# Attention probabilities: the far high parts copied behind the exponentials, and no work held back behind the last unit

## The chip, the cores and the metric

The kernel runs on one core of one Trainium2 chip. Its metric is the device time of one execution in microseconds. Before the change three timed executions gave 1129.56, 1130.15 and 1130.64 us; their median, 1130.15 us, is the time before. The core's engines are TensorE (PE for products and transposes, PEld for its weight loads), VectorE (DVE), ScalarE (ACT), GpSimd (POOL) and SyncE (SP, which issues most DMAs).

## The reference, cut to what matters

One encoder layer over 1024 tokens of width 1024, batch 1, in float32. It begins with an RMSNorm and one projection into a pooling part (512 columns) and queries, keys and values of 8 heads of 64. The change lies in the chunked attention:

```python
def one_chunk(args):
    c, qb = args                                   # 64 queries; keys: own chunk and 8 before
    s = jnp.einsum('bqhd,bkhd->bhqk', qb, kb).astype(jnp.float32) * scale + bias
    s = jnp.where(valid[None, None, None, :], s, -jnp.inf)
    pr = jax.nn.softmax(s, axis=-1).astype(vb.dtype)
    return jnp.einsum('bhqk,bkhd->bqhd', pr, vb)
```

Behind it come the output projection with its residual, a gated MLP (width 2816, with a causal convolution), a gated per-layer embedding and a last RMSNorm; none of these is touched.

## The kernel before, in words

**Precision.** Every product of two float32 operands is made of three products of reduced ones: an operand is split into a high part (a rounding copy on ACT) and a low part (the operand less its high part, on DVE), and high x high, high x low and low x high are summed in PSUM (`mm3`, lines 136 to 138; `split`, lines 141 and 142). Here "copy" means the making of a high part and "remainder" the making of a low part.

**Units.** Attention runs per pair of heads (4 pairs) and per unit of query tiles of 128 tokens. A pair has 6 units: tiles 0 to 2 together, then tiles 3, 4, 5, 6 and 7 alone, so there are 24 units. A tile sees up to 5 key tiles; the units have 6, 4, 5, 5, 5 and 5 key tiles.

**Visits.** `unit(u)` is called for u = 0 to 24. I call it visit u, and number it within its round of six: visit 0 works on the scores of tiles 0 to 2, visit 1 on tile 3, up to visit 5 on tile 7. On PE a visit issues, in this order:

1. the transposes of the probabilities of unit u-1 (line 441, `probs_t`);
2. the scores of unit u (line 418);
3. steps of a long projection that fills the time (queries and keys of the next pairs, then the pooling columns: `project`, generator `fill`; a step is one `mm3`);
4. in the visits after the last tile of a group (tiles 0 to 2, 3 to 5, 6 and 7), the products of probabilities and values of that group (line 493, `values`). These are visits 1, 4 and 0, and visit 24; the code calls them valued. Visit 0 is also called merged here, since its own unit has three tiles.

**PSUM.** There are 8 banks. Transposed probabilities of the first four key tiles of a unit go to banks 2 and 3, those behind the fourth (the far ones) to banks 6 and 7: two key tiles for the unit of tiles 0 to 2, none for tile 3, one for each of tiles 4 to 7. Scores lie in banks 4 to 7: a tile with four or five key tiles uses all four of them. Projections use banks 0 and 1, the values bank 5 and one of banks 0 and 1.

**ACT and DVE.** Their work of a visit is not issued where it is written. `push(t, fn)` puts it on a list with a time t, and `flush` issues the list in order of t; both engines then work in exactly this order, each through its own queue. Entries that are marked slow (weight splits of the projection and splits of queries and keys) stay on the list when `flush(True)` is called and go out with the next plain `flush()`. The entries are:

- the copy of the transposed probabilities (line 459, ACT) at 0.0 for near, 0.05 for far ones;
- per head and tile the minimum of the negated scores plus bias (lines 383 and 387, DVE) from 1.0 on, the exponential with its sum (line 395, ACT) from 1.9 to 3.3, the reciprocal (line 398, DVE) from about 2.95, and the scaled row (line 391 on ACT for the second head of the pair, from 3.9; line 393 on DVE for the first, from 3.0);
- the remainder of the probabilities (line 461, DVE) at 2.5 (near) and 2.52 (far) in valued visits, at 3.55 and 3.57 in the others;
- the evacuation of a finished projection bank (lines 300 and 584, DVE), at the time it is finished, though not before 3.6 in visits that are not valued;
- slow entries at 5.2 or later (lines 329, 332, 330, 333; weight splits: copy line 529 on ACT, remainder line 527 on DVE or POOL).

The next visit's transposes write the banks that the remainders read, so they follow the remainders of this visit. Within a group the value products take the key tiles in the order wide, narrow, wide and so on, first all high parts, then all low parts; in the group of tiles 3 to 5 the far key tile of tile 5 comes second, in the group of tiles 0 to 2 a far key tile comes second too, in the group of tiles 6 and 7 the far key tile of tile 7 comes fourth.

**The end.** Visit 24 has no unit of its own: it transposes and copies the probabilities of unit 23, issues nine projection steps, then the values of unit 23. Behind them the projection goes on with the second half of the last column block's weights (`weights(ct, 1)`), whose split is a slow entry. The order in which ACT and DVE work is that of the code; the work that follows the attention (output weights, splits of its result) lies partly between. Output weights (line 640, SP) are loaded into the buffers from which the projection weights are split.

Of the kernel before, what the change touches and what calls it, by code (L numbers as in the profile page):

```python
# [8 lines left out]
AF = mybir.ActivationFunctionType  # L9
# [66 lines left out]
NU = len(UNITS)  # L76
PER = NU // (N_HEADS // 2)


def key_tiles(u):  # L80

    return sum(min(t + 1, BANDT) for t in UNITS[u][1]) if 0 <= u < NU else 0


def group_at(t):

    return next(g for g in GROUPS if g[0] <= t < g[1])


def is_last(u):  # L90

    t = UNITS[u][1][-1]
    return t + 1 == group_at(t)[1]


def block_at(k, t):

    t0, t1 = group_at(t)
    return t1 * t + k if t0 == 0 else 5 * (t - t0) + k - t + 4 - max(0, 4 - t0)


def trunk(tc, xT, xn, pT, vecs, w_qk0, w_in, w_v, bias, counts, pool_w, w_out, w_up, w_down,
          w_gate, w_ple, out):
    nc = tc.nc
    act, dve, pe, pool, sp = nc.scalar, nc.vector, nc.tensor, nc.gpsimd, nc.sync

    with tc.tile_pool(name="sb", bufs=1) as sb, \
# [23 lines left out]
        def rv(ap):  # L131
            return ap.bitcast(F32)
# [172 lines left out]
        def push(t, *fns, slow=False):  # L305

            for n, fn in enumerate(fns):
                pending.append((t + 0.8 * n, len(pending), fn, slow))

        def flush(part=False):  # L310
            todo = sorted((p for p in pending if not (part and p[3])), key=lambda p: p[:2])
            pending[:] = [p for p in pending if part and p[3]]
            owed.clear()
            for p in todo:
                p[2]()
# [21 lines left out]
        def run_later(n):  # L337
            for fn in later[:n]:
                fn()
            del later[:n]  # L340
# [26 lines left out]
        def load_bias(h):  # L367
            b = biasb[h % 3]
            sp.dma_start(b, bias[h])

            def turned():
                dve.memset(b[0:64, 576:640], -BIG)
                dve.memset(b[64:128, 0:64], -BIG)
            return turned
# [53 lines left out]
        def probs_t(u):  # L428

            c, ts = UNITS[u]  # L430
            total = key_tiles(u)

            def place(x, m):
                n = 2 * m + x
                return (2, HD * n) if n < 8 else (6, 512 + HD * (n - 2 * total))

            for x in range(2):
                for m in range(total):
                    bank, col = place(x, m)
                    for y in range(2):  # L440
                        pe.transpose(PS[:, bank + y, col:col + HD], Sb[x][halves[y], m * P:(m + 1) * P],  # L441
                                     ident[halves[y], halves[y]], tile_position=(HD * y, 0))
            todo, m = [], 0
            for t in ts:
                nk = min(t + 1, BANDT)
                b0 = block_at(t + 1 - nk, t)
                for a, b in ((0, min(nk, 4 - m)), (max(4 - m, 0), nk)):
                    if b > a:
                        bank, col = place(0, m + a)
                        todo.append((b0 + a, b0 + b, bank, PS[:, bank:bank + 2, col:col + 2 * HD * (b - a)]))  # L450
                m += nk
            return todo

        def probs_out(todo, valued):
            for a, b, bank, ps in todo:
                src = ps.rearrange("p a (n q) -> p n a q", q=HD)
                hi, lo = [pt[:, a:b].rearrange("p k x (a q) -> p (k x) a q", a=2) for pt in PT]
                far = bank > 3
                push(0.05 if far else 0.0, lambda hi=hi, src=src: act.activation(hi, src, AF.Copy))  # L459
                push((2.5 if valued else 3.55) + 0.02 * far,  # L460
                     lambda lo=lo, src=src, hi=hi: dve.tensor_tensor(lo, src, rv(hi), ALU.subtract))  # L461

        credit, turns, valued = 0.0, [], [False]

        def values(u):
            nonlocal credit
            c_, ts = UNITS[u]
            if not is_last(u):
                return
            t0, t1 = group_at(ts[-1])  # L470
            n, by = t1 - t0, 4 if t0 else t1
            while u < NU - 1 and at[0] < 2.3:
                next(fill)
                credit -= 0.5
                now[0] += STEP
            flush(True)
            reach = {k: (max(t0, k), min(t1, k + BANDT)) for k in range(max(0, t0 - 4), t1)}
            wide = [k for k, (a, b) in reach.items() if b - a == n]
            narrow = sorted((k for k in reach if k not in wide), key=lambda k: reach[k][1] - reach[k][0])
            keys = [k for pair in zip(wide, narrow) for k in pair]  # L480
            keys += [k for k in wide + narrow if k not in keys]
            free = (bankn[0] + 1) % 2
            if n == 2:
                bank = free if u < NU - 1 else 5
                Os = [PS[:, bank, 256 * j:256 * j + 256] for j in range(2)]
            else:
                Os = [PS[:, bank, 0:n * P] for bank in (5, free)]
            todo = [(part, k) for part in range(2) for k in keys]
            for j in range(2):
                for n_, (part, k) in enumerate(todo):  # L490
                    a, b = reach[k]
                    b0 = block_at(k, a)
                    pe.matmul(Os[j][:, (a - t0) * P:(b - t0) * P].rearrange("p (t q) -> p t q", q=P), V[:, k, 2 * c_ + j],  # L493
                              PT[part][:, b0:b0 + by * (b - a - 1) + 1:by, j], start=n_ == 0, stop=n_ == len(todo) - 1)
            for j in range(2):
                a = halves[j]
                act.activation(otmp[a, 0:n * P], Os[j][halves[1 - j]], AF.Copy)  # L497
                if n == 2 and j == 0:
                    continue
                for i in range(2) if n == 2 else (j,):  # L500
                    a = halves[i]
                    dve.tensor_tensor(o32[a, c_, t0 * P:t1 * P], Os[i][a], otmp[a, 0:n * P], ALU.add)
                if j == 0:
                    flush()
# [167 lines left out]
        def lay_due(u):  # L672

            for c, x, h in list(qk_ready):
                if u >= (c - 1) * PER + (0 if x else PER - 1 if h else 1):
                    qk_ready.remove((c, x, h))
                    push(max(4.8, now[0] + 0.4), *lay(c, x, h), slow=True)
# [4 lines left out]
        def unit(u):  # L682

            nonlocal credit
            now[0] = 0.0
            unit_at[0] = u
            if u < NU:
                c, ts = UNITS[u]
                for h in range(2 if ts[-1] > 3 else 1):
                    while not all((c, x, h) in laid for x in range(2)):  # L690
                        next(fill)
                        lay_due(u - 1)
                        flush()
            valued[0] = u > 0 and is_last(u - 1)
            if u:
                probs_out(probs_t(u - 1), valued[0])
            if u < NU:
                softmax(scores(u), valued[0])
                if u % PER == PER - 1:
                    for h in (2 * c + 3, 2 * c + 4):  # L700
                        if h < N_HEADS:
                            push(3.0, lambda h=h: turns.append(load_bias(h)))
                lay_due(u)
                credit += ROOM[u % PER]
                now[0] = 1.25
                least = LEAST[u % PER] if u else 0
                while credit >= 1 or least > 0:
                    if valued[0] and credit < 2 and least < 1 and 4.7 < at[0] < 5.4:
                        break
                    now[0] += STEP  # L710
                    credit -= 1
                    least -= 1
                    if next(fill, True) is False:
                        break
                    lay_due(u)
            else:
                for _ in range(DRAIN):
                    now[0] += STEP
                    next(fill)
            if valued[0]:  # L720
                flush(True)
                values(u - 1)
            flush()
            if turns and (u % PER == PER - 1 or u % PER == 1):
                turns.pop(0)()
            run_later(LATER)
# [766 lines left out]
```

## Time and profile before

| what | value |
|---|---|
| timed executions | 1129.56, 1130.15, 1130.64 us; median 1130.15 us |
| the profiled execution's own time | 1126.68 us |
| its span, first to last instruction | 1124.9 us |
| granted TensorE clock | 0.998 |
| busy: PE, PEld, DVE, ACT, POOL | 1109.0, 919.9, 842.8, 579.9, 163.5 us |
| attention, from the first scores to the last values | about 71 to 262 us of the span |

All rows of the trace are of the profiled execution. A row of a timeline has the start in us from the span's beginning, the duration in us, engine, line, operation and operands; in square brackets stands how long the engine had been idle before it and what ended that. A row of waits has the engine, its line, what it waited for, the total in us, the number of times, and the longest. A row of groups has the number of instructions, the total in us and the mean of one in ns.

### The profile page before, as it was taken

The page shows a single profiled execution, that of the slowest core. Times are in us where ns is not written, and L with a number is a line of the kernel's source. Part 1 is how long each engine was busy: PE and PEld are TensorE (multiplying, and loading weights), DVE is VectorE, ACT ScalarE, POOL GpSimd, SP SyncE. Part 2 cuts the span into 40 slices and gives each one's busy share as a digit, 9 for nine tenths or more (in the row PEclk, how much of TensorE's full clock was granted, in tenths as well). Part 3 has the DMA queues.
Part 4 walks back from the last instruction along what each step waited for, and adds up shares of the span by engine and source line. Part 5 has one row for each costly group of instructions (what it writes and reads, how often), then busy time and mean ns, then how long its engine had stood idle before and what let it go on. Part 6 is the DMA issues. An engine that isn't in the chain of part 4 may idle for free.

```text
span 1124.9 us, 15599 instructions
## 1 busy us (share of the span) xinstructions
PE 1109.0 (99%) x5658; PEld 919.9 (82%) x5658; DVE 842.8 (75%) x1449; ACT 579.9 (52%) x1021; POOL 163.5 (15%) x196
## 2 busy tenths in 40 slices
PE   9999999999999999999999999999999999999997
PEld 7888877877888888888888888888888888888887
DVE  6437777777668879887787778778877789986845
ACT  7537766664564544444443444344444544674634
POOL 0000101086002200210112011201120112000000
PEclk9999999999999999999999999999999999999999
DMA  9401111103510352674668465756576556420003
GB/s 346 160 1 38 44 43 39 41 20 129 176 52 10 92 163 92 159 169 131 159 150 177 133 160 140 170 149 159 136 166 157 132 156 133 142 94 20 1 31 119
DMA packets 66172, 129.02 MB, mean 115 GB/s; under 512 B 7600, under 2 KB 9008, under 8 KB 66096
## 3 DMA queue, kind: packets, MB, share of 16 engines
q1 hardware_dynamic: 51840, 102.33, 27.5%
q0 software_dynamic: 13824, 25.17, 13.9%
q8 instruction: 44, 0.72, 0.3%
q10 hardware_dynamic: 432, 0.53, 0.1%
q14 instruction: 32, 0.26, 0.1%
HBM read 113.32 MB, written 14.68 MB: 114 GB/s over the span
## 4 chain that ended last, share of the span: by engine, by line
PE 84%; DVE 7%; ACT 5%; issue 3%; POOL 1%; POOLq 0%; DVEq 0%; ACTq 0%
PE PS L136 26%; PE PS L137 26%; PE PS L138 26%; PE PS L493 3%; ACT F L395 2%; DVE B L461 2%; ACT B L459 1%; DVE F L383 1%; DVE R L142 1%; PE PS L441 1%; PE PS L418 1%; ACT R L141 0%; POOL TB L951 0%; POOL F L941 0%; ACT F L497 0%
## 5 line engine op out<-in xcount | busy, mean ns | idle before, releaser
L136 PE MATMUL PS<-R 128*128 128x512 f32 (+1 forms) x1084 | 420.1, 388 | 0.1
L138 PE MATMUL PS<-R 128*128 128x512 f32 (+1 forms) x1084 | 416.9, 385 | 0.0
L137 PE MATMUL PS<-R 128*128 128x512 f32 (+1 forms) x1084 | 416.9, 385 | 0.0
L136 PEld LDWEIGHTS PS<-R 128*128 128x128 f32 x1084 | 203.6, 188 | 44.0 <-issue 2.9
L138 PEld LDWEIGHTS PS<-R 128*128 128x128 f32 x1084 | 203.6, 188 | 40.8
L137 PEld LDWEIGHTS PS<-R 128*128 128x128 f32 x1084 | 203.7, 188 | 39.5
L141 ACT ACTIVATE R<-F 128x512 fp32r<-128x512 f32 (+2 forms) x220 | 136.6, 637 | 174.6 <-PE PS L137 78.4
L142 DVE TENSOR_TENSOR R<-F,R 128x512 fp32r<-128x512 f32 (+2 forms) x220 | 152.4, 709 | 46.9 <-ACT R L141 45.9
L876 DVE TENSOR_TENSOR F<-F 128x512 f32<-128x512 f32 x88 | 60.7, 690 | 51.1 <-DMA F<-in_w_up 50.3
L1186 DVE TENSOR_TENSOR F<-F,PS 128x512 f32<-128x512 f32 x140 | 92.8, 683 | 6.6 <-PE PS L138 6.4
L141 ACT ACTIVATE BQ<-RW 128x512 fp32r<-128x512 f32 x90 | 52.6, 622 | 76.7 <-PE PS L137 72.5
L1129 POOL DMA_DIRECT2D RW<-Yd x56 | 49.5, 885 | 260.9 <-DMA RW<-Yd 196.9
L1129 POOL DMA_DIRECT2D RW<-in_w_down x40 | 35.9, 945 | 231.6 <-DMA RW<-in_w_down 195.2
L142 DVE TENSOR_TENSOR BQ<-RW,BQ 128x512 fp32r<-128x512 f32 x90 | 59.2, 688 | 2.5 <-PE PS L137 1.7
L137 PE MATMUL PS<-BQ 128*128 128x512 f32 x140 | 54.6, 390 | 0.1
L138 PE MATMUL PS<-BQ 128*128 128x512 f32 x140 | 54.5, 389 | 0.0
L136 PE MATMUL PS<-R,BQ 128*128 128x512 f32 x140 | 54.5, 389 | 0.0
L136 PE MATMUL PS<-BQ 128*128 128x512 f32 x140 | 54.5, 389 | 0.0
L137 PE MATMUL PS<-R,BQ 128*128 128x512 f32 x140 | 54.5, 389 | 0.0
L138 PE MATMUL PS<-R,BQ 128*128 128x512 f32 x140 | 54.5, 389 | 0.0
L1012 ACT ACTIVATE F<-F,vec 128x1024 f32<-128x1024 f32 (+1 forms) x25 | 28.6, 1143 | 48.5 <-DVE F L987 43.6
L395 ACT ACTIVATE F<-F,small 128x640 f32<-128x640 f32 (+4 forms) x64 | 43.9, 689 | 18.2 <-DVE small L383 17.0
(179 smaller groups left out, 1581.3 us busy)
## 6 DMA issues: line engine op xcount, KB each, us to landing
F<-in_w_up SPq DMA_DIRECT2D x91, 256.0 KB, 4.2
RW<-Yd SPq DMA_DIRECT2D x60, 256.0 KB, 3.7
RW<-Yd POOLq DMA_DIRECT2D x56, 256.0 KB, 4.8
RW<-in_w_down SPq DMA_DIRECT2D x50, 256.0 KB, 3.0
RW<-in_w_down POOLq DMA_DIRECT2D x40, 256.0 KB, 6.2
Yd<-F SPq DMA_DIRECT2D x40, 256.0 KB, 3.5
F<-in_w_in SPq DMA_DIRECT2D x10, 512.0 KB, 3.5
F<-in_xn SPq DMA_DIRECT2D x8, 512.0 KB, 7.2
```

Of the source, the lines that this page charges most:

```text
L136: pe.matmul(ps, ahi, bhi, start=first, stop=False, skip_group_check=more)
L137: pe.matmul(ps, ahi, blo, start=False, stop=False, skip_group_check=more)
L138: pe.matmul(ps, alo, bhi, start=False, stop=last, skip_group_check=more)
L141: both = (act.activation(hi, src, AF.Copy), dve.tensor_tensor(lo, src, rv(hi), ALU.subtract))
L142: dve.tensor_tensor(lo, src, rv(hi), ALU.subtract))
L395: push(1.9 + 0.85 * z, lambda S=S, s_=s_: act.activation(S, S, AF.Exp, bias=s_[:, 0:1], scale=-1.0, accum_out=s_[:, 1:2]))
L461: lambda lo=lo, src=src, hi=hi: dve.tensor_tensor(lo, src, rv(hi), ALU.subtract))
L493: pe.matmul(Os[j][:, (a - t0) * P:(b - t0) * P].rearrange("p (t q) -> p t q", q=P), V[:, k, 2 * c_ + j], PT[part][:, b0:b0 + by * (b - a - ...
L876: return dve.tensor_tensor(rawu[to], rawu[a], rawu[b], op)
L1012: act.activation(y, Gb[:, 2 + a:2 + b], AF.Identity, bias=vec[:, C_CB + fi:C_CB + fi + 1], scale=cw(2))
L1129: pool.dma_start(t, src, accum_op=ALU.add)
L1186: dve.tensor_tensor(t, t, PS[:, 4 + d], ALU.subtract if n in (1, 5) else ALU.add)
```

## The change

In `probs_out` the copies and remainders of far probabilities get other times; near ones keep theirs. In a valued visit the far copy moves from 0.05 to 2.92, which is behind both exponentials of a single tile (1.9 and 2.75), and in a merged visit to 2.76, which is behind the fourth of six exponentials (2.75). The far remainder goes from 2.52 to 0.01 behind its copy. In the other visits the far copy moves to 3.5, behind the exponentials and ahead of the scaled row on ACT, and its remainder stays at 3.57. In `values` and in `unit`, the `flush(True)` ahead of the value products becomes a plain flush for the last unit, so that its slow entries are issued ahead of them.

```diff
-        def probs_out(todo, valued):
+        def probs_out(todo, valued, merged):
             for a, b, bank, ps in todo:
                 src = ps.rearrange("p a (n q) -> p n a q", q=HD)
                 hi, lo = [pt[:, a:b].rearrange("p k x (a q) -> p (k x) a q", a=2) for pt in PT]
                 far = bank > 3
-                push(0.05 if far else 0.0, lambda hi=hi, src=src: act.activation(hi, src, AF.Copy))
-                push((2.5 if valued else 3.55) + 0.02 * far,
+                soon = 2.76 if merged else 2.92
+                push(0.0 if not far else soon if valued else 3.5, lambda hi=hi, src=src: act.activation(hi, src, AF.Copy))
+                push((soon + 0.01 if valued else 3.57) if far else 2.5 if valued else 3.55,
                      lambda lo=lo, src=src, hi=hi: dve.tensor_tensor(lo, src, rv(hi), ALU.subtract))
...
-            flush(True)
+            flush(u < NU - 1)
...
-                probs_out(probs_t(u - 1), valued[0])
+                probs_out(probs_t(u - 1), valued[0], u % PER == 0)
...
             if valued[0]:
-                flush(True)
+                flush(u < NU)
                 values(u - 1)
```

The first of the two flushes is in `values(u)`, where u is the unit whose values are made (23 for the last), the second in `unit(u)`, where the last visit is 24.

## The prediction

> **What bounds the kernel now.** I began with the page and the busy time by stage.
>
> ```profile
> span 1124.9 us, 15599 instructions
> ...
> PE 84%; DVE 7%; ACT 5%; issue 3%; POOL 1%; POOLq 0%; DVEq 0%; ACTq 0%
> ```
>
> ```profile
> 71.00:262.00 191.00, 185.01 (x1480) 153.10 (x1478) 136.44 (x349) 127.39 (x268) 47.30 (x63) 1.00 0.13 41
> 262.00:285.00 23.00, 21.38 (x93) 17.41 (x94) 18.69 (x33) 13.42 (x23) 8.56 (x12) 1.00 0.32 103
> ```
>
> In each row stand the stretch, its length, then busy time of PE, PEld, DVE, ACT and POOL, clock, DMA share and GB/s. PE sets the end: 84% of the chain of waits is PE. In the stretch of the attention it is idle for 191.00 - 185.01 = 6.0 us, in the 23 us behind it for 1.6 us. These 7.6 us are all that moving ACT and DVE work can win there, and what PE wins there it should keep, since it is the bound of what follows. The longest waits of the weight loads, and one of DVE, between 55 and 285 us say where the idle time is:
>
> ```profile
> PEld PS L441 <- DVE B L461: 9.2, 12, 1.3
> ```
>
> ```profile
> DVE F L383 <- ACT B L459: 19.6, 16, 3.0
> ```
>
> PE waits for the remainders (L461) when it starts the transposes of a visit (and once behind the last values, shown below). The second row shows who is late before that: the minimum waits for the probability copy 16 times. Sixteen is the number of visits with a far copy and scores that fill banks 4 to 7 (visits 1, 3, 4, 5 in four rounds).
>
> **The far copy and the minimum.** Visit 2 has no far copy; the next visit has one:
>
> ```profile
> 85.92 1.12 PE L418 MATMUL PS<-R 64*128 64x320 f32 x12
> 86.16 1.03 ACT L459 ACTIVATE B<-PS 128x1024 fp32r<-128x1024 f32 x1 [0.16 <-PE PS L441]
> 87.08 0.82 DVE L383 CUSTOM_DVE_ANT_0 F<-PS,F 128x640 f32<-128x640 f32 x1 [0.46 <-PE PS L418]
> ...
> 136.82 1.13 PE L418 MATMUL PS<-R 64*128 64x320 f32 x12
> 137.41 0.69 DVE L330 TENSOR_TENSOR R<-F,R 128x512 fp32r<-128x512 f32 x1 [0.70 <-ACT R L329]
> 137.80 1.28 ACT L459 ACTIVATE B<-PS 128x1024 fp32r<-128x1024 f32 x2
> 139.12 0.82 DVE L383 CUSTOM_DVE_ANT_0 F<-PS,F 128x640 f32<-128x640 f32 x1 [1.01 <-ACT B L459]
> 143.09 0.14 PEld L441 LDWEIGHTS PS<-ident,F 64*128 64x128 f32 x2 [1.26 <-DVE B L461]
> ```
>
> At 87.08 the minimum starts 0.04 behind the end of the scores (85.92 + 1.12), while the near copy still runs (to 87.19): a near copy does not hold it. At 139.12 it starts behind the end of the second copy (137.80 + 1.28 = 139.08), though the scores ended at 137.95 and DVE was free at 138.10. So the far copy costs this minimum 139.12 - 138.12 = 1.0 us, and all that hangs on it (exponentials, reciprocals, remainders, the next transposes) as much.
>
> [...]
>
> **Visits 3 and 5** (not valued). What can PE win at the next visit's start? A wait of 0.35 us stands ahead of transposes even where no remainder is late:
>
> ```profile
> 77.41 0.70 PEld L441 LDWEIGHTS PS<-ident,F 64*128 64x128 f32 x20 [0.35 <-issue]
> ...
> 136.17 0.14 PEld L441 LDWEIGHTS PS<-ident,F 64*128 64x128 f32 x2 [0.84 <-DVE B L461]
> ...
> 185.72 0.20 PEld L441 LDWEIGHTS PS<-ident,F 64*128 64x128 f32 x4 [1.25 <-DVE B L461]
> ```
>
> Of the 9.2 us in 12 waits, 12 x 0.35 = 4.2 can't be won. The two last rows are starts of visit 3: they follow a visit 2, which has no far copy, and their excess (0.49 + 0.90 = 1.4) stays; the other two of this kind are at the floor. That leaves 9.2 - 4.2 - 1.4 = 3.6 us in eight waits behind visits 3 and 5. The wait shown at 143.09 has an excess of 0.91 and its minimum can advance by 1.0. One behind a visit 5:
>
> ```profile
> 152.65 1.13 PE L418 MATMUL PS<-R 64*128 64x320 f32 x12
> ...
> 154.24 0.82 DVE L383 CUSTOM_DVE_ANT_0 F<-PS,F 128x640 f32<-128x640 f32 x1 [1.05 <-ACT B L459]
> ...
> 158.22 0.78 PEld L441 LDWEIGHTS PS<-ident,F 64*128 64x128 f32 x20 [0.55 <-DVE B L461]
> ```
>
> The minimum can start at 153.78 + 0.04, 0.42 earlier; the excess is 0.20. In both the advance is larger than the excess, so nearly all goes: I take **3.4 us**, upper bound 3.6.
>
> What the moved copy costs there is hidden. The groups of remainders (four key tiles) and of far copies (one and two key tiles):
>
> ```profile
> L461 DVE TENSOR_TENSOR B<-PS,B 128x1024 fp32r<-128x1024 f32 x20 | 24.2, 1209 | 0.0
> ...
> L459 ACT ACTIVATE B<-PS 128x256 fp32r<-128x256 f32 x24 | 9.1, 380 | 0.3 <-PE PS L418 0.3
> ...
> L459 ACT ACTIVATE B<-PS 128x512 fp32r<-128x512 f32 x8 | 4.8, 601 | 0.0
> ```
>
> A copy of 0.38 us now stands ahead of the second head's scaled row on ACT. That row goes back by 0.38 at most, against an advance of 0.42 or more, and only transposes of the second head need it, which come ten transposes behind the first. The far remainder stays behind the near one, whose 1.21 us are longer than the copy. With this cover gone and no advance the eight copies would cost 8 x 0.38 = 3.0 us, the lower bound.
>
> **Valued visits.** In visits 1 and 4 the copy goes behind both exponentials, and the value products read that block second. Visit 4 of the third round:
>
> ```profile
> 196.77 2.51 PE L493 MATMUL PS<-B,R 128*128 128x384 f32 x13
> 196.86 0.19 ACT L395 ACTIVATION_READ_ACCUMULATOR F<-F,small 128x1 f32 x1
> 197.81 1.32 PEld L493 LDWEIGHTS PS<-B,R 128*128 128x128 f32 x8 [0.27 <-DVE B L461]
> ```
>
> With the minimum 0.42 earlier (the figure of visit 5, which has the same scores), ACT is through its sums at 197.05 - 0.42 = 196.63 and through the far copy at 197.01. The second value product would start at 196.77 + 2.51/13 = 196.96: it waits some 0.1. In exchange the near remainder is 0.42 earlier and the wait of 0.27 at 197.81 goes. On DVE the far remainder now waits for its copy, with the reciprocals and the scaled row queued behind it; the near remainder ahead (1.21 us) covers most or all of that. In merged visits the copy delays the last two of six exponentials by 0.38; reciprocals there stand behind remainders on DVE anyway. Bounds: a gain of 8 x 0.27 = 2.2, a loss of 4.8 (below). I take **0.1 us**: the shown visit nets 0.17, and a visit whose values come later nets nothing either way.
>
> **The end.** The last values and what follows:
>
> ```profile
> 258.83 2.96 PE L493 MATMUL PS<-B,R 128*128 128x256 f32 x24
> 261.82 0.77 ACT L497 ACTIVATE F<-PS 64x256 f32<-64x256 f32 x2 [3.03 <-PE PS L493]
> 262.62 0.63 ACT L529 ACTIVATE B<-F 128x512 fp32r<-128x512 f32 x1
> 263.30 0.50 PE L136 MATMUL PS<-R,B 128*128 128x512 f32 x1 [1.51 <-ACT B L529]
> 263.51 0.78 DVE L527 TENSOR_TENSOR B<-F,B 128x512 fp32r<-128x512 f32 x1
> 264.35 0.50 PE L138 MATMUL PS<-R,B 128*128 128x512 f32 x1 [0.32 <-DVE B L527]
> ```
>
> ACT idles 3.03 us waiting for the values while a weight copy of 0.63 stands behind; PE then waits for that copy and its remainder, 1.51 + 0.32 = 1.83 us. With everything issued ahead both run in that idle time and PE goes on. I take **1.9 us** (1.8 by idle time, up to 2.1 by the pace of the products); the lower bound is 0, since the split only moves into ACT's idle 3.03 us, and the gain is lost if something else is late there. The buffers that the remainder frees, which output weights wait for, come free earlier too, so no load becomes late.
>
> **The sum.** 3.4 + 0.1 + 1.9 = 5.4 us. The profiled execution, 1126.68 us (span plus 1.78), would become 1121.3. It lies 3.5 below the median of the timed runs; the same 5.4 off 1130.15 gives **1124.8 us**. The upper bounds add up to 3.6 + 2.2 + 2.1 = 7.9, the lower ones to a loss of 3.0 + 4.8 = 7.8.
>
> **Rivals.** *Only the end pays.* The remainders come earlier, but something else of the visit, the scaled rows or the projection bank's evacuation, holds PE as long. For it: the excess of a wait is under 1 us, and other work of the visit ends close by. Against it: the row of 12 waits names L461 alone. Time: 1130.15 - 1.9 = 1128.2.
>
> *Slower: the value products wait for far copies.* Place: second value product in visits 1 and 4. If the exponentials did not advance, the copy in the visit above would end at 197.05 + 0.38 = 197.43, 0.5 behind the 196.96 at which it is wanted; where two key tiles are far (visit 1, 0.60 us) 0.7. Four of each lose 4.8 us, the end gives back 1.9: 1133.0. It decides from an advance under 0.35 us; the row at 87.08, where nothing far stands ahead, speaks against that.
>
> *No change.* The far copy waits no less but elsewhere (order turned round, 16 times, each gain met by a wait of the values), and the end's stall goes to a load: 1130.
>
> **How the numbers follow.** The forecast gets 0.77, including a larger gain; only the end 0.11; no change 0.05; slower 0.07. Between 0.2% (2.26 us) either way a measurement of this kernel hardly tells a difference: the first is faster, the second and third the same, the fourth slower. The range holds the forecast with its bounds and reaches to the end-only case: 1121.8 to 1128.4; left out are no change, slower, and some of the large gains, under 0.2 together.
>
> **What would show it.** Right: L383 waits for L418 or for nothing, not for L459; L441's wait for L461 falls from 9.2 to about 5.8; no wait of PE for L529 behind the last values; L459 far copies behind L395. Wrong: a new wait of L493 for L459 over 1 us in total; L441 waiting for L391; PE idle behind 262 us as before.

## The result and the profile after

The changed kernel took 1118.65 us, the median of five executions (1117.71 to 1120.03), against 1129.56 us of the kernel before, measured beside it (five, 1127.68 to 1130.64): a ratio of 0.9905, 95% interval 0.9891 to 0.9919, so 9.2 to 12.3 us faster. The forecast was 1124.8, with a range from 1121.8 to 1128.4. The sign was right; the time lies 3.2 us below the range.

The page of the changed kernel has the span and the shares of the chain of waits (its own time was 1118.21 us):

```profile
span 1116.4 us, 15614 instructions
...
PE 89%; DVE 5%; issue 2%; ACT 2%; POOL 1%; POOLq 0%; DVEq 0%; ACTq 0%
```

The busy times by stage, for the attention and for the stretch behind it (columns as in the prediction):

```profile
71.00:258.00 187.00, 184.59 (x1493) 154.33 (x1492) 139.53 (x353) 130.07 (x275) 49.21 (x64) 1.00 0.14 45
258.00:280.00 22.00, 22.00 (x99) 18.23 (x98) 20.88 (x34) 13.46 (x21) 10.32 (x11) 1.00 0.30 90
```

PE is idle for 187.00 - 184.59 = 2.4 us in the attention, where it was 6.0, and no longer idle behind it, where it was 1.6. Idle time isn't the whole gain, though. From the start of visit 1 to that of visit 24, before and after:

```profile
77.41:251.73 174.32, 168.54 (x1370) 139.63 (x1370) 125.86 (x319) 120.00 (x248) 37.60 (x49) 1.00 0.11 36
```

```profile
78.09:245.97 167.88, 165.47 (x1370) 138.47 (x1370) 125.53 (x319) 119.08 (x248) 37.83 (x49) 1.00 0.12 38
```

PE works off 1370 products in both. Its idle time falls by 3.4 us (5.8 to 2.4), and the time that counts as busy falls by another 3.1. The waits of the weight loads and of DVE between 55 and 285 us:

```profile
PEld PS L441 <- DVE B L462: 5.8, 12, 1.3
...
PEld PS L494 <- ACT F L391: 1.2, 1, 1.2
...
PEld PS L494 <- ACT B L460: 0.6, 3, 0.2
```

```profile
DVE F L383 <- PE PS L418: 10.1, 9, 2.2
```

Lines behind the edit are one higher here: 460 is the copy, 462 the remainder, 494 the value products. The minimum (L383) waits for the scores alone, no longer for a copy; the starts of the visits wait 5.8 us for remainders, where it was 9.2; and there is a small new wait of the value products for far copies, 0.6 us in three times.

**Where the time went.** I cut the span at two points that PE reaches in both kernels: the transposes that open visit 24, and the norm sums of the MLP (line 804, now 805). Rows of the timeline before, then after; the first transposes of visit 1 before stand in the prediction (77.41):

```profile
251.73 0.34 PE L441 MATMUL PS<-ident,F 64*128 64x64 f32 x4 [0.45 <-DVE B L461]
...
326.37 0.41 PEld L804 LDWEIGHTS PS<-small,F 128*128 128x128 f32 x2
```

```profile
78.09 0.33 PEld L441 LDWEIGHTS PS<-ident,F 64*128 64x128 f32 x8 [0.35 <-issue]
...
245.97 0.40 PE L441 MATMUL PS<-ident,F 64*128 64x64 f32 x6
...
318.21 0.19 PEld L805 LDWEIGHTS PS<-small,F 128*128 128x128 f32 x1
```

Visits 1 to 23 take 251.73 - 77.41 = 174.3 us before and 245.97 - 78.09 = 167.9 after: 6.4 less. From there to the norm sums it is 74.6 and 72.2: 2.4 less. Behind that 0.3 is gained and ahead of visit 1 0.7 lost, where the change touches nothing. Together 8.5 us, which is the difference of the two profiled executions (1126.68 - 1118.21).

The first number can be split by kind of visit: a visit lasts from the start of its transposes to that of the next. In after's timeline each of the four visits 3 lasts 6.01 us, where they lasted 6.70, 6.92, 6.41 and 6.48. Summed over the rounds, in us:

| visit | before | after | less |
|---|---|---|---|
| 3 | 26.51 | 24.04 | 2.5 |
| 5 | 25.18 | 24.17 | 1.0 |
| 1 (valued) | 32.80 | 31.75 | 1.05 |
| 4 (valued) | 35.11 | 34.11 | 1.0 |
| 0 (valued, three in the cut) | 28.88 | 28.52 | 0.4 |
| 2 | 25.84 | 25.29 | 0.6, all in round 2 |

### The profile page after: what moved, and what is told of

It reads as the page before. It is cut to its first block, busy times and chain, and to the rows that moved or that the text cites. A ratio compares the mean times of both kernels' runs of the same rounds, so it can differ in the third digit from the quotient of the medians.

```text
span 1116.4 us, 15614 instructions
## 1 busy us (share of the span) xinstructions
PE 1105.7 (99%) x5658; PEld 919.7 (82%) x5658; DVE 846.4 (76%) x1449; ACT 579.6 (52%) x1021; POOL 167.1 (15%) x196
## 4 chain that ended last, share of the span: by engine, by line
PE 89%; DVE 5%; issue 2%; ACT 2%; POOL 1%; POOLq 0%; DVEq 0%; ACTq 0%
PE PS L136 28%; PE PS L137 27%; PE PS L138 27%; PE PS L494 3%; PE PS L418 2%; PE PS L441 1%; DVE R L142 1%; DVE B L462 1%; ACT F L395 1%; ACT R L141 0%; DVE F L383 0%; POOL TB L952 0%; POOL F L942 0%; PE PS L226 0%; PE PS L211 0%
```

## The experiments

All ratios are to the kernel before, on the same chip. "Attention" is the time from the start of visit 1 to that of visit 24, "tail" from there to the norm sums, both from the timeline. In two executions of the same kernel the attention agreed within 0.06 us (before 174.32 and 174.38, after 167.88 and 167.93), so it tells far smaller things apart than the whole time does.

| kernel | timed ratio, 95% | attention | tail |
|---|---|---|---|
| before again | 0.9995 (0.9986 to 1.0004) | 174.4 | 76.3 |
| after again | 0.9916 (0.9902 to 0.9930) | 167.9 | 72.2 |
| the end alone | 0.9965 (0.9951 to 0.9980) | 174.4 | 72.2 |
| far parts alone | 0.9946 (0.9933 to 0.9959) | 167.9 | 74.7 |
| far copy, visits not valued | 0.9960 (0.9948 to 0.9972) | 170.2 | 74.5 |
| far copy and remainder, valued visits | 0.9979 (0.9969 to 0.9989) | 171.5 | 74.7 |
| remainder alone, valued visits | 1.0002 (0.9993 to 1.0010) | 174.3 | 76.2 |
| far copy just ahead of the exponentials | 1.0021 (1.0012 to 1.0029) | 177.1 | 76.2 |
| slow entries behind both halves of the values | 0.9925 (0.9913 to 0.9938) | 168.6 | 72.2 |
| one more remainder on POOL | 0.9908 (0.9893 to 0.9923) | 167.3 | 72.3 |
| both of these | 0.9921 (0.9909 to 0.9934) | 168.8 | 72.5 |
| far parts alone, longer stall at the end | 0.9957 (0.9945 to 0.9970) | 167.9 | 77.9 |

**The end alone.** The two flushes of the change, nothing else.

```diff
-            flush(True)
+            flush(u < NU - 1)
...
-                flush(True)
+                flush(u < NU)
```

> Only the plain flush ahead of the last values; all copies as before. Theory (the parts add, each in its own visits): PE no longer waits for the weight split behind the last values, 2.2 to 2.4 us less than before (ratio 0.998); the waits of the minimum for the copy (19.6 us, 16 times) and of the transposes (9.2 us, 12 times) stay. Rival (the stall of the end only pays once the visits are shorter, because something else is late there): under 1 us.

The tail falls by 2.4 us, from 74.64 in the first profile of before; attention, and the waits of the minimum (19.5 us) and of the transposes (9.2), stay. So the two parts of the change can be taken apart.

**The far parts alone.** The edit of `probs_out` and its call.

> The far copies and remainders moved as in the change; the flush as before. Theory: 6.5 us less span than the profiled execution of before (7 to 8.5 us in timed runs), the wait behind the last values stays at 1.8 us. Rival (the two edits need each other): under 5 us.

The attention is that of the changed kernel (167.88), the tail that of before (74.66). The parts add up: 6.4 + 2.4. So do the timed ratios: 0.35% for the end and 0.54% for the far parts, against 0.84 to 0.95% for both. The timed gain of the far parts, about 6 us, is less than the 7 to 8.5 that I had expected.

**Only the visits that are not valued.**

```diff
-                push(0.05 if far else 0.0, lambda hi=hi, src=src: act.activation(hi, src, AF.Copy))
+                push(0.0 if not far else 0.05 if valued else 3.5, lambda hi=hi, src=src: act.activation(hi, src, AF.Copy))
```

> Only the far copies of visits 3 and 5 moved (to 3.5); valued visits and the end as before. Theory: 3.4 us in the starts of visits 4 and 0, and up to 0.6 from transposes that no longer pause for the far remainder: 3.5 to 4 us. Rival (the gains seen in valued visits come from these visits): 6 us or more.

**Only the valued visits**, with the remainder's new time (`merged` is passed as in the change).

```diff
+                soon = 2.76 if merged else 2.92
-                push(0.05 if far else 0.0, lambda hi=hi, src=src: act.activation(hi, src, AF.Copy))
+                push(0.0 if not far else soon if valued else 0.05, lambda hi=hi, src=src: act.activation(hi, src, AF.Copy))
-                push((2.5 if valued else 3.55) + 0.02 * far,
+                push((soon + 0.01 if valued else 3.57) if far else 2.5 if valued else 3.55,
```

> Only the far copies of visits 1, 4 and 0 moved (behind the exponentials); visits 3 and 5 and the end as before. My prediction: 0.1 us. Theory now, from the two traces: 2.5 to 3 us, in the value products of visits 1 and 4 (0.3 to 0.4 in five of eight) and the scores of one visit 2. Rival (those gains come from visits 3 and 5): under 1 us, or slower, since the values then wait for the copies.

The waits of DVE, first of the kernel without valued visits, then of the one with them alone:

```profile
DVE F L383 <- ACT B L459: 11.6, 8, 3.0
```

```profile
DVE F L383 <- ACT B L460: 8.4, 8, 1.7
```

Of the 16 waits of the minimum for a copy each kernel keeps eight. The unvalued half takes 4.1 us from the attention: visit 3 2.5, visit 5 1.1, and 0.3 each at visits 4 and 0, which follow them. The valued half takes 2.8: visit 1 1.0, visit 4 0.7, visit 2 0.55, and 0.6 in the visits 3 and 5 of round 4 that the first half wins as well. With two decimals that is 4.14 + 2.84 - 0.58 = 6.40, and the joint gain is 6.44. So the valued visits add 2.3 us to what the others win, where I had 0.1.

**Is it the copy or the remainder?** The copy keeps its time, the far remainder takes that of the change (`merged` passed as there).

```diff
+                soon = 2.76 if merged else 2.92
-                push((2.5 if valued else 3.55) + 0.02 * far,
+                push((soon + 0.01 if valued else 3.57) if far else 2.5 if valued else 3.55,
```

> Only the far remainder of the valued visits moved (2.93 and 2.77); all copies as before. This tells whether the gain of valued visits is the copy's (the minimum and exponentials earlier) or the remainder's (the projection bank evacuated ahead of it). Theory: the copy's; so here 0 to 0.6 us, in the two visits 1 in which the evacuation is due between 2.5 and 2.9. Rival: 2 us or more.

Waits of the weight loads in it:

```profile
PEld PS L494 <- DVE B L462: 2.3, 5, 1.0
```

Attention 174.3: nothing (the minimum waits for the copy 19.6 us in 16 times, as before). Visit 1 loses 0.4 (the value products now wait for the late far remainder), visits 2 and 3 win as much. So the later remainder alone wins nothing, and the gain of the valued visits needs the copy's move. The remainder has to follow its copy, so the copy alone can't be run.

**Is it the bank, or just the load on ACT?** In visits 3 and 5 the far copy goes to a place between those of before and after: on ACT just ahead of the exponentials.

```diff
-                push(0.05 if far else 0.0, lambda hi=hi, src=src: act.activation(hi, src, AF.Copy))
+                push(0.0 if not far else 0.05 if valued else 1.85, lambda hi=hi, src=src: act.activation(hi, src, AF.Copy))
```

> Far copies of visits 3 and 5 at 1.85: issued behind both minima and ahead of both exponentials; all else as before. Theory (the order is by bank: minimum and far copy share banks 6 and 7): the copy can't run before the second minimum is done, so the first exponential starts about 1.1 us less the minimum's advance (0.4 to 1.0) later than before; 3 to 5 us slower than before. Rival (the minimum only waits for ACT's place in the order, not for a bank): the copy runs right behind the near one, the minimum at the end of the scores, and the kernel gains 3.5 us as with the copy at 3.5.

Waits of ACT and of the weight loads:

```profile
ACT B L459 <- DVE small L383: 11.0, 8, 1.6
```

```profile
PEld PS L441 <- DVE B L461: 12.0, 12, 1.3
```

The order has turned round, as the change does it, but at a place where it hurts: the copy waits eight times for the second minimum, both exponentials stand behind it, and the transposes wait 12.0 us instead of 9.2. Attention is 2.7 us longer, somewhat less than I had expected, and the time 0.12 to 0.29% longer. The rival, a gain of 3.5 us, is refuted. The minima themselves win as much as in the changed kernel, so a minimum that no longer waits is worth nothing where the exponentials then wait for the copy. The copy reads banks 6 and 7, which the two minima read too, and starts when the second one is done: in one visit 3 that minimum ends at 139.26 + 0.82 = 140.08 and the copy starts at 140.12, after ACT had been idle for 0.81 us; over the eight visits these waits are the 11.0 us. So it isn't the load on ACT that sets the order. Why the two reads keep apart, no run here shows.

**Before and after once more**, for what differs between executions of one kernel.

> The kernel before once more, for a second trace. The profiled execution of before took 1126.68 us, less than each of its five timed ones (1127.68 to 1130.64), while that of the changed kernel (1118.21) lies at its median. Theory (the first trace caught a fast execution of before, and the change takes away what differs): span 1126.5 to 1128.5 and more PE idle time in the attention than the 6.0 us of the first trace. Rival (the trace is as good as any, and the timed runs have something that no trace has): span 1124.9 within 0.5 again.

> The changed kernel once more. Theory: 10.5 to 11 us less than before in timed runs, span within 1 us of 1116.4. Rival: a gain nearer 8.5, the difference of the first two traces.

Both gave their attention again, and after its tail; before's tail was 1.6 us longer than in its first profile. My theory of a longer attention of before in a second trace is refuted, though its span, 1128.1 us, lies where I had it. After's second span, 1121.9 us, is 5.4 longer than its first, where I had expected 1 at most; 5.0 of that lie behind the norm sums. Both are told below.

**Can more be had?** One wait that is left is that of the value products for the second head's scaled row (1.2 us, once), with DVE work queued ahead of the reciprocals. Three tries on top of the changed kernel: slow entries issued behind both halves of the values instead of between them, one more weight remainder moved from DVE to POOL, and both.

```diff
-                    flush()
+                    flush(True)
```

```diff
-                    (pool if name[0] in (4 + 1, 8 + 2, 4 + 2, 8 + 3, 2) else dve).tensor_tensor(lo, src, rv(hi), ALU.subtract)
+                    (pool if name[0] in (4 + 1, 8 + 2, 4 + 2, 8 + 3, 4 + 3, 2) else dve).tensor_tensor(lo, src, rv(hi), ALU.subtract)
```

> The changed kernel, and slow entries go out behind the evacuation of both halves of the values instead of between them. Theory (starts of visit 3 still wait up to 1.26 us because visit 2 begins late: a weight split and a query split run between the two evacuations on ACT and DVE): the split moves but DVE does the same work ahead of the minimum, so 0 to 0.7 us in the attention; rival (the order between the evacuations sets it): 1.5 us, all the excess of the three waits.

> The changed kernel, with the weight remainders of one more column block (the keys' and queries' block 7) on POOL instead of DVE. Theory (DVE is what makes the second round's visit 0 and the third round's visit 2 late): 0.7 us or so in that visit 0, whose values wait 1.2 us, and up to 0.7 in that visit 2; rival (POOL's remainder takes 1.3 us against 0.7 on DVE, and PE then waits for weights): slower by up to 1 us.

> Both of these edits on the changed kernel. Theory: the sum or more, 1.5 to 2.5 us less attention time than the changed kernel, some 11 to 12 us less than before in timed runs. Rival (each is hidden by the other): no more than the better one.

The first makes visit 2 of round 4 longer and the attention 0.7 us longer, where I had expected a gain. The second halves the wait, against a new one for POOL; the weight loads' waits in it:

```profile
PEld PS L494 <- ACT F L391: 0.6, 1, 0.6
PEld PS L138 <- POOL B L528: 0.4, 1, 0.4
```

Its attention is 0.6 us shorter than that of the changed kernel, and its time is 1118.0 us (1117.5 to 1119.18). It beats before, and by the attention in its one trace the changed kernel too; the timed ratios (0.9908 against 0.9905 and 0.9916) can't tell the two apart. Both together make the attention 0.9 us longer than the changed kernel's, against theory and rival alike; why is not shown.

**The end made worse.** The far parts alone, and the first copy of each value half done twice behind the last values, so that PE waits longer there; the second copy writes the same again.

```diff
-                act.activation(otmp[a, 0:n * P], Os[j][halves[1 - j]], AF.Copy)
+                for _ in range(2 if u == NU - 1 else 1):
+                    act.activation(otmp[a, 0:n * P], Os[j][halves[1 - j]], AF.Copy)
```

> Far copies moved as in the change, the flush as before, and the copies of the last values made twice (same result), so that the stall behind the last values is 0.76 us longer. In three of the seven traces with that stall TensorE then ran at half its pace for 3.4 us, which cost 1.6 us more. Theory (the stall itself lets the clock fall): granted clock under 0.9 between 255 and 270 us, and 2.3 to 2.5 us more between the last transposes and the first norm than the 74.6 us of undisturbed traces. Rival (the clock falls by chance): 75.4 us and clock 1.0.

The tail is 3.2 us longer than with the far parts alone, though PE's wait for the weight copy is only 0.8 longer (2.33 against 1.51 us), and its second wait (0.31 us) no longer shows as idle time. I had expected 2.3 to 2.5 more, not 3.2. The rest is in the section on the hardware.

## Why the prediction was right in its direction and wrong in its size

**The ceiling: a premise that failed.** "These 7.6 us are all that moving ACT and DVE work can win there." The attention and the tail won 6.4 + 2.4 = 8.8. The 7.6 counted PE's idle time alone. By the two windows of the first section (1370 products each), 3.1 us of the attention's gain lie in time that counts as busy. Where products wait for their weight loads within a run of products, the run's row grows longer and shows no idle time. Two such runs stand below: the values of a visit 4, 4.07 against 3.77 us, and the scores of a visit 2, 1.59 against 1.13.

**Visits 3 and 5: right.** Predicted 3.4 us, measured 2.5 + 1.0 = 3.5. The wait of L441 for remainders was to fall to about 5.8 and is 5.8. How it went, in visit 3 of round 2, from after's timeline:

```profile
135.86 1.01 ACT L460 ACTIVATE B<-PS 128x1024 fp32r<-128x1024 f32 x1
...
136.07 0.82 DVE L383 CUSTOM_DVE_ANT_0 F<-PS,F 128x640 f32<-128x640 f32 x1
...
138.57 0.36 ACT L460 ACTIVATE B<-PS 128x256 fp32r<-128x256 f32 x1
...
138.78 1.54 DVE L462 TENSOR_TENSOR B<-PS,B 128x1024 fp32r<-128x1024 f32 x2
...
140.23 0.84 PE L441 MATMUL PS<-ident,F 64*128 64x64 f32 x20
```

The minimum starts during the near copy (135.86 to 136.87); the far copy ends at 138.93 and is hidden behind the near remainder, as I had it. But one thing was left out: in both kernels the remainders of the two parts go out together (x2), and before the transposes behind them took 0.92 us, with a pause in the middle for the far one; now they take 0.84 (the last row above). Before:

```profile
158.22 0.92 PE L441 MATMUL PS<-ident,F 64*128 64x64 f32 x20
```

Visits 4 and 0, which begin with these transposes, win 0.06 to 0.09 each where only the unvalued visits are changed. One of them, visit 0 of round 3, wins 0.23 (the wait of its values for the scaled row falls as well, from 1.3 to 1.2 us), and the last one nothing; it is 0.6 us in all. With it the unvalued half makes up its 4.1.

**Valued visits: the step that failed.** "I take 0.1 us: the shown visit nets 0.17, and a visit whose values come later nets nothing either way." Measured 2.3 us, just above the upper bound of 2.2. Even the shown visit was undervalued. Its value products before, and the same place in after's timeline:

```profile
196.77 4.07 PE L493 MATMUL PS<-B,R 128*128 128x384 f32 x24
```

```profile
192.26 1.54 DVE L462 TENSOR_TENSOR B<-PS,B 128x1024 fp32r<-128x1024 f32 x2
...
192.67 0.36 ACT L460 ACTIVATE B<-PS 128x256 fp32r<-128x256 f32 x1
...
192.91 3.77 PE L494 MATMUL PS<-B,R 128*128 128x384 f32 x24
193.08 3.32 PEld L494 LDWEIGHTS PS<-B,R 128*128 128x128 f32 x23 [0.21 <-ACT B L460]
```

The loads wait 0.21 for the far copy, the loss I had foreseen, but the 24 products take 3.77 us instead of 4.07: they win 0.30, not 0.17. The visits that I had set to nothing won most. Visit 1 of round 2, and the visit 2 that follows it, before and after:

```profile
127.31 2.10 PE L493 MATMUL PS<-B,R 128*128 128x384 f32 x12
127.59 0.68 DVE L300 TENSOR_TENSOR F<-PS,F 128x512 f32<-128x512 f32 x1
...
128.32 0.88 PEld L493 LDWEIGHTS PS<-B,R 128*128 128x128 f32 x6 [0.25 <-DVE F L300]
...
128.43 0.72 ACT L391 ACTIVATE F<-F,small 128x512 f32<-128x512 f32 x1 [1.68 <-DVE small L398]
...
129.86 1.59 PE L418 MATMUL PS<-R 64*128 64x320 f32 x12
...
130.31 0.88 PEld L418 LDWEIGHTS PS<-R 64*128 64x128 f32 x11 [0.29 <-DVE F L502]
```

```profile
124.62 0.68 DVE L300 TENSOR_TENSOR F<-PS,F 128x512 f32<-128x512 f32 x1
125.22 0.68 DVE L462 TENSOR_TENSOR B<-PS,B 128x512 fp32r<-128x512 f32 x1
...
126.13 0.72 ACT L391 ACTIVATE F<-F,small 128x512 f32<-128x512 f32 x1 [1.26 <-DVE small L398]
126.23 1.79 PE L494 MATMUL PS<-B,R 128*128 128x384 f32 x12
...
128.47 1.13 PE L418 MATMUL PS<-R 64*128 64x320 f32 x12
```

Before, the second head's values wait 0.25 for the projection bank to be evacuated (L300, ending at 128.27), with both remainders ahead of it on DVE; after, the far remainder is behind it (125.22), and the evacuation is done at 125.30, before the values begin. And before, ACT does a late scaled row (L391) ahead of the value evacuation (L497), so the scores of visit 2 wait 0.29 for what follows from that (L502); after, the row is through ahead of the values' end and the scores run without a pause. I had asked only whether the far copy would come in time for the value products. I hadn't asked what else is queued behind the minimum on ACT and DVE, and PE waited for that. Summed over the rounds: visit 1 1.05, the value products of visit 4 0.7 (the 1.0 of the table less 0.3 for the transposes), visit 2 of round 2 0.55; 2.3 in all.

**The end: mis-sized.** "I take 1.9 us (1.8 by idle time, up to 2.1 by the pace of the products)." Measured 2.4. The products behind the values, before and after (timelines):

```profile
263.63 0.40 PE L137 MATMUL PS<-R,B 128*128 128x512 f32 x1
...
264.69 0.40 PE L136 MATMUL PS<-R,B 128*128 128x512 f32 x1
```

```profile
253.07 2.96 PE L494 MATMUL PS<-B,R 128*128 128x256 f32 x24
...
255.87 0.40 PE L136 MATMUL PS<-R,B 128*128 128x512 f32 x1
...
256.56 0.39 PE L136 MATMUL PS<-R,B 128*128 128x512 f32 x1
```

From the end of the values to the start of the fourth product it was 264.69 - 261.79 = 2.90 us; it is 256.56 - 256.03 = 0.53. Idle time counts from the end of the last product. What it misses is twofold. Without a stall a product starts ahead of the end of the one before it (255.87 against 256.03), and each stall loses that. And a product behind a stall is followed by the next after 0.33 us (263.30 and 263.63) instead of 0.23 (after, 256.33 and 256.56). Two stalls cost 1.83 us of idle time and 0.54 of overlap.

**From the profile to the median: a step that failed.** "It lies 3.5 below the median of the timed runs; the same 5.4 off 1130.15." After, the profiled execution lies only 0.4 below the median. The other 3.0 us of the miss lie here, as much as in the trace (8.5 against 5.4). Two parts can be named. The 3.5 was in part the sample: it rests on a median of three executions, 1130.15, while 67 later ones of before (some on another chip) have a median of 1128.7. Against those the profiled execution lies 2.0 below, and only one of the 67 was faster; that the first trace was of so fast an execution was luck. The other part is a drop of the clock behind the stall at the end (last section), which the first profile of before happened not to have and which the change does away with. The rest stays open: the two profiles of after differ by 5.0 us behind the norm sums, where no edit reaches. About 3.4 of these are one wait of PE in the MLP and the clock behind it (last section).

**The rivals.** *Only the end pays* is refuted by the far parts alone (0.9933 to 0.9959). *The value products wait for far copies*: the place was right, the price 0.6 us in three waits and not 4.8, since the minima did advance. *No change* fell with the ratio. Of the signs named, all those of a right forecast came. Of those of a wrong one, only the wait of the value products for the copy is there, at 0.6 us, under the 1 that I had set.

## What to carry to other kernels

When an engine's queue is freed by some time, follow everything behind the freed point in that queue to the next places where the bound engine waits, in each kind of stage, and don't set those you haven't opened to nothing: here the ones I hadn't opened held as much as the end. Don't take the idle time of the bound engine as the most that can be won: nearly half of the attention's gain came out of time that counted as busy. Price a stall by the distance of PE's starts on both sides of it, rather than by its idle time. And before carrying a difference between the profile and the median over to the changed kernel, ask whether the change removes what makes it, and whether the median rests on enough executions.

## What the runs showed of the hardware

Behind a stall of PE of 1.83 us (two waits) the granted clock fell in some executions, which cost another 1.6 us (the difference of two tails, below). The second profile of before has the same two waits behind the last values as the first (1.51 and 0.32 us). Its timeline and its windows there (the clock is the third column from the end):

```profile
263.57 0.50 PE L136 MATMUL PS<-R,B 128*128 128x512 f32 x1 [1.51 <-ACT B L529]
...
264.61 0.51 PE L138 MATMUL PS<-R,B 128*128 128x512 f32 x1 [0.32 <-DVE B L527]
...
265.19 0.58 PE L137 MATMUL PS<-R,B 128*128 128x512 f32 x1
...
268.55 0.45 PE L136 MATMUL PS<-R,B 128*128 128x512 f32 x1
```

```profile
262.00:266.00 4.00, 2.17 (x8) 1.41 (x8) 1.62 (x3) 1.39 (x3) 3.61 (x6) 0.90 0.21 63
266.00:270.00 4.00, 4.00 (x14) 3.15 (x13) 2.08 (x3) 2.75 (x6) 3.76 (x6) 0.67 0.24 63
```

From 265.19 to 268.55 eight products start 0.42 us apart instead of 0.23: about 3.4 us at half pace, 1.5 lost, at a granted clock of 0.90 and 0.67 in the two windows. With half the clock where it was low, as the pace of the starts suggests, these means make it 2 x (0.10 x 4 + 0.33 x 4) = 3.4 us, an estimate that agrees with the 3.4 us of slow starts. The first profile of before has the clock at 1.00 in this stretch (the row in the prediction), and that is nearly the whole difference of their tails (76.28 - 74.64 = 1.64). With the longer stall of the last experiment:

```profile
256.00:262.00 6.00, 4.15 (x9) 2.98 (x10) 1.58 (x3) 2.18 (x5) 5.37 (x10) 0.60 0.15 52
262.00:266.00 4.00, 4.00 (x15) 3.20 (x14) 3.79 (x6) 4.00 (x8) 2.09 (x3) 0.74 0.52 157
```

Here products start at least 0.4 us apart from 257.85 to 264.11, most of them 0.43. The same estimate from the clocks of these windows, 0.60 and 0.74, gives 2 x (0.40 x 6 + 0.26 x 4) = 6.9 us; the slow starts make up 6.3 of them, so some 0.6 would fall into the stall. Of the 3.2 us of longer tail 0.8 are stall, about 2.4 clock. And the second profile of after, which has no stall at the end, has such a stretch in the MLP. PE waits 1.8 us there (its weight loads 2.2) for ACT (L964), and the clock is 0.83 in place of 1.00:

```profile
680.00:690.00 10.00, 8.21 (x30) 6.26 (x29) 3.44 (x6) 2.80 (x6) 1.75 (x2) 0.83 0.71 194
```

The two waits at the end, 1.83 us together, have such a stretch behind them in some executions and not in others: the first and the second profile of before have the same waits, with clocks of 1.00 and 0.67 from 266 to 270 us. What decides it, no run here shows.

How often: half pace for 3.4 us lowers the mean clock of an execution by 0.0015 (0.5 x 3.4 / 1128). Of 111 executions of kernels that have the stall at the end 72 have a mean granted clock of 0.997 or less, of 31 without it 1, and of the five with the longer stall all. At 1.5 us in two thirds of the executions this would be, as an estimate, 1.0 us of the mean, on top of the 8.5 that the two first profiles differ by; the timed difference was 9.2 to 12.3. The times agree: of the 67 later executions of before, the 46 at 0.997 or less have a median of 1129.0 us, the other 21 one of 1128.1. The mean can't say where in an execution the clock fell; I read the place from the traces alone: of the seven profiles of kernels with the short stall three show it behind the last values (tails of 76.2 to 76.3 us in the table, against 74.5 to 74.7 in the other four). Nor is it shown what the clock did in the other stretches of the timed executions.
